# Forgetting attention in pairs of short and long query blocks, products in groups of four banks, TensorE order pinned

## Chip, core and metric

One Trainium2 chip (trn2); the program runs on one of its cores. The metric is the device time of one execution in microseconds (us), median of the runs. A difference of 0.2% (5 us) is about what a measurement of this kernel can tell from no change.

## The reference, cut to what matters

A decoder layer: a hybrid mixer (forgetting attention beside a gated linear attention), cross-attention into 256 memory tokens, a mixture of experts. The change is in the forgetting attention alone: 8 heads of 64 columns over 2048 positions, in float32.

```python
c = jnp.cumsum(log_sigmoid(f_logit), axis=-1)
for blk in range(S // 128):
    q0, q1 = blk * 128, blk * 128 + 128
    s = einsum('bhqd,bhkd->bhqk', q[:, :, q0:q1], k[:, :, :q1]) * d ** -0.5
    s = s + c[:, :, q0:q1, None] - c[:, :, None, :q1]
    p = softmax(where(causal, s, -inf), axis=-1)
    outs.append(einsum('bhqk,bhkd->bhqd', p, v[:, :, :q1]))
```

Query block qb (0 to 15) looks at (qb+1)*128 keys, so the work of a block grows sixteenfold over a head.

## The kernel before, in words

The program is a chain of stages. Stage 1 projects the input and leaves queries and keys in DRAM (`fqk_d`), the cumulated gates in `c_d`, values in `fv_d`. Stage 2 (`stage2`, from L456) is the forgetting attention. Stage 3 projects the result, and so on to the experts.

The order of instructions on each engine is not that of the source: a scheduler of the framework simulates the program and fixes one order per engine. Only what is marked `tc.keep_in_program_order` keeps its source order on its engine. Buffers (`bufs=n`) rotate, so an instruction that writes a tile waits for the last reader of the n-th tile before it.

Per head, `prep(h)` loads the head's queries `q2` and keys `k2` twice (both partition halves, [128,2048], L474, L475) and the gates `cr`, broadcast (L477); every second head the values of two heads (L482). In four chunks of 512 columns it splits queries and keys into high and low parts: R on ScalarE (L486) and VectorE (L487), L1 on ScalarE (L489), L2 on GpSimd (L490). R is triple-buffered, L1, L2 and cr double, q2 and k2 single. `prep` of head h+2 is started when head h ends.

Per query block, `scores` goes over banks of 512 keys: two matmuls R x L1 and R x L2 (L506, L507), on the last bank a third one that adds the causal mask (L509), into one of three PSUM banks `ps_s`. VectorE subtracts cr, takes the running maximum and writes the bank to SBUF (`sc`, five buffers of [128,2048]; L510); it negates the maximum (L515); ScalarE takes the exponentials in pieces of up to 1024 columns, with their sums (L518).

Per pair of query blocks, `values` goes over banks of two key blocks: up to four transposes into one of three PSUM banks `pt` (L536); the evacuation `t`, two of three on ScalarE (L541), one on VectorE (L539); then up to four products (L529) with the values (64 columns) as stationary operand, the two query blocks in the two column halves of the array, into `po`. The products of a bank are issued after the transposes of the next one. `close` copies `po` (L553, ScalarE), adds the sums and takes their reciprocal (L556, L557, L559), transposes back (`pn`, L562) and multiplies (L564); at the end of a head the normalisation goes over GpSimd (L571, L576) and out by DMA (L577).

Blocks are taken in order 0 to 15, head after head; the scores run four blocks ahead (`AHEAD = 4`), spread over the banks of `values` by a ratio of costs. From the fourth head on, free slots are given to `memory_in`, the preparation of the cross-attention (L744 to L774).

Of the kernel before, what the change touches and what calls it, by code (L numbers as in the profile page):

```python
# [25 lines left out]
def f32(ap):  # L26
    return ap.bitcast(F32)
# [18 lines left out]

def skip(gen, n):
    """gen, after n empty steps"""
    for _ in range(n):
        yield  # L50
    yield from gen


class Trunk:
# [9 lines left out]
    def split(self, hi, lo, src, scale=None):  # L64
        """hi + lo = src (* scale), each exact in a float32r"""
# [8 lines left out]
    def rstd(self, out, ss, mul, pool, eps=EPS, tag=""):  # L74
        """out = (ss * mul + eps) ** -0.5"""
# [19 lines left out]
    def consts(self):  # L95
# [8 lines left out]
        # -1e30 above the diagonal (row q, column k > q)  # L104
# [5 lines left out]
        with self.tc.tile_pool(name="vrows", bufs=1) as rp, self.tc.tile_pool(name="ps_c", bufs=1, space=PSUM) as pp:  # L110
# [10 lines left out]
            # blank lists for the routing  # L121
# [7 lines left out]
    def stage1(self):  # L129
# [3 lines left out]
        with tc.tile_pool(name="xT", bufs=1) as xp, tc.tile_pool(name="w1", bufs=2) as wp, \  # L133
                tc.tile_pool(name="ps1", bufs=2, space=PSUM) as pp:
            xh, xl = zip(*[[xp.tile([128, KT, 512], F32R, name=f"x{n}{c}") for n in "hl"] for c in range(4)])
            # the narrow columns: forget logits at 0..7, GLA gate inputs at 32..47
# [22 lines left out]
            def ttype(ws, m, c, dst):  # L159
                """rows m*128.. of the group's transposed product, tokens of chunk c"""  # L160
# [21 lines left out]
            with tc.tile_pool(name="xin", bufs=2) as ip, tc.tile_pool(name="psx1", bufs=2, space=PSUM) as px:  # L182
                xn = [[] for _ in range(4)]

                def prenorm(c):
                    """load and normalise chunk c"""
# [11 lines left out]
                def turn(c):  # L198
                    """chunk c transposed: yields after each bank"""
# [10 lines left out]
                def narrow(c):  # L210
# [6 lines left out]
                    # c: the running sum of log sigmoid(forget logit)  # L217
# [110 lines left out]
    def gla(self, gp, pp):  # L328
# [19 lines left out]
        for g in range(S // G):  # L348
# [3 lines left out]
            for p in range(2):  # L352
# [9 lines left out]
                # log decay, summed within chunks (16 times the reference's, taken off in the exps)  # L362
# [29 lines left out]
                # scores within chunks, level by level  # L392
# [13 lines left out]
                # within blocks of 8: factors of both signs about the block's middle, bounded as each  # L406
                # step's decay is held at exp(-17), under a float32's resolution beside the diagonal
# [10 lines left out]
                # between the halves of blocks of 2h, about the first half's end  # L418
# [28 lines left out]
                # the queries' factor 1/8 is in here: (o / 8) / sqrt(mean(o^2) / 64 + eps)  # L447
# [9 lines left out]
    def stage2(self):  # L457
        nc, tc = self.nc, self.tc
        with tc.tile_pool(name="fx", bufs=1, reuse_waits="tile") as fp, \
                tc.tile_pool(name="psx", bufs=2, space=PSUM, reuse_waits="tile") as pp:  # L460
            vs, heads, n_evac = {}, {}, [0]
            # in the order in which the last head lets go of them, for the stage that follows
            big = {}
            for nm in ("q2", "k2", "R0", "L10", "L20", "cr0", "R2", "R1", "L11", "L21", "cr1"):
                big[nm] = lambda nm=nm: fp.tile([128, S], F32R if nm[0] in "RL" else F32, name=nm)
            XW = 1024

            def prep(h):
                if h >= 8:
                    return  # L470
                q2, k2 = big["q2"](), big["k2"]()
                dma = nc.sync.dma_start if h == 1 else nc.gpsimd.dma_start
                for d in (slice(0, 64), slice(64, 128)):
                    dma(q2[d], self.fqk_d[h])  # L474
                    dma(k2[d], self.fqk_d[8 + h])  # L475
                R, L1, L2, cr = big[f"R{h % 3}"](), big[f"L1{h % 2}"](), big[f"L2{h % 2}"](), big[f"cr{h % 2}"]()
                dma(cr, bcast_rows(self.c_d, S, h * S))  # L477
                # [q hi; q lo] over 8 against [k hi; k hi] and [k lo; k lo]
                heads[h] = R, L1, L2, cr
                if h % 2 == 0:  # L480
                    v = vs[h // 2] = fp.tile([128, NT, 128], F32, name="v", bufs=2)
                    nc.gpsimd.dma_start(v, self.fv_d[:, h * 64:h * 64 + 128].rearrange("(b k) d -> k b d", k=128))  # L482
                yield
                for c in range(4):
                    cs = slice(c * 512, (c + 1) * 512)
                    nc.scalar.activation(R[:, cs], q2[:, cs], AF.Copy, scale=0.125)  # L486
                    nc.vector.scalar_tensor_tensor(R[64:128, cs], q2[64:128, cs], 0.125, f32(R)[64:128, cs], op0=OP.mult, op1=OP.subtract)  # L487
                    yield
                    nc.scalar.activation(L1[:, cs], k2[:, cs], AF.Copy)  # L489
                    nc.gpsimd.tensor_tensor(L2[:, cs], k2[:, cs], f32(L1)[:, cs], OP.subtract)  # L490
                    yield

            def scores(u):
                """exp(s - max) of head h's query block, and its sums: yields after each bank"""
                h, qb = u["h"], u["qb"]
# [3 lines left out]
                sc = u["P"] = fp.tile([128, S], F32, name="sc", bufs=5)  # L499
                m = fp.tile([128, 5], F32, name="m", bufs=4)  # L500
                for i, c0 in enumerate(range(0, n, 512)):
# [4 lines left out]
                    nc.tensor.matmul(ps[:, :w], R[:, qs], L1[:, ks], start=True, stop=False)  # L506
                    nc.tensor.matmul(ps[:, :w], R[:, qs], L2[:, ks], start=False, stop=not diag)  # L507
                    if diag:
                        nc.tensor.matmul(ps[:, w - 128:w], self.identb, self.cmask, start=False, stop=True)  # L509
# [6 lines left out]
                for j, c0 in enumerate(range(0, n, XW)):  # L516
                    cs = slice(c0, min(n, c0 + XW))
                    nc.scalar.activation(sc[:, cs], sc[:, cs], AF.Exp, bias=m[:, 4:5], accum_out=u["l"][:, j:j + 1])  # L518
                yield

            def values(u0, u1):
                """the outputs of two query blocks, transposed, in the array's two column halves:
                yields after each bank"""
                qb, po = u0["qb"], u1["po"]
                v, d = vs[u0["h"] // 2], slice(u0["h"] % 2 * 64, u0["h"] % 2 * 64 + 64)

                def product(t, todo):
                    for i, (half, kb) in enumerate(todo):
                        nc.tensor.matmul(po[half * 64:half * 64 + 64], v[:, kb, d], t[:, i], start=kb == 0, stop=kb == qb + half)  # L529

                last = None
                for g0 in range(0, qb + 1, 2):
                    todo = [(half, kb) for kb in (g0, g0 + 1) for half in range(2) if kb <= qb + half]
                    pt = pp.tile([128, 4, 128], F32, name="pt", bufs=3)
                    for i, (half, kb) in enumerate(todo):
                        nc.tensor.transpose(pt[:, i], (u0, u1)[half]["P"][:, kb * 128:(kb + 1) * 128], self.ident)  # L536
                    t = fp.tile([128, 4, 128], F32, name="t", bufs=4)
                    if n_evac[0] % 3 == 1:
                        nc.vector.tensor_copy(t[:, :len(todo)], pt[:, :len(todo)])  # L539
# [1066 lines left out]
```

## Time and profile before

| what | value |
|---|---|
| three runs | 2484.33, 2485.76, 2489.12 us (median 2485.76) |
| profiled execution, span | 2482.5 us |
| TensorE (PE) busy | 2368.5 us, 95% |
| VectorE (DVE) busy | 1444.0 us, 58% |
| ScalarE (ACT) busy | 1087.4 us, 44% |
| GpSimd (POOL) busy | 451.5 us, 18% |
| DMA, mean | 133 GB/s |
| stage 2: first score matmul to last product | 728.74 to about 1227 us |

The span is the time from the first to the last instruction of one profiled execution; no other time is given for that execution, and it stands 3.3 us below the median of the runs. Matmuls are pipelined, so their durations in the timeline overlap: what a group of matmuls takes is read from the start of one row to the start of the next. PEclk is the granted clock of TensorE as a share of its full speed (2.4 GHz); its lower level is 1.2 GHz.

### The profile page before, as it was taken

The page shows a single profiled execution, that of the slowest core. Times are in us where ns is not written, and L with a number is a line of the kernel's source. Part 1 is how long each engine was busy: PE and PEld are TensorE (multiplying, and loading weights), DVE is VectorE, ACT ScalarE, POOL GpSimd, SP SyncE. Part 2 cuts the span into 40 slices and gives each one's busy share as a digit, 9 for nine tenths or more (in the row PEclk, how much of TensorE's full clock was granted, in tenths as well). Part 3 has the DMA queues.
Part 4 walks back from the last instruction along what each step waited for, and adds up shares of the span by engine and source line. Part 5 has one row for each costly group of instructions (what it writes and reads, how often), then busy time and mean ns, then how long its engine had stood idle before and what let it go on. Part 6 is the DMA issues. An engine that isn't in the chain of part 4 may idle for free. (4 is left out here: it accounts for less than half of the span.)

```text
span 2482.5 us, 46191 instructions
## 1 busy us (share of the span) xinstructions
PE 2368.5 (95%) x17849; PEld 2022.0 (81%) x17849; DVE 1444.0 (58%) x4096; ACT 1087.4 (44%) x2438; POOL 451.5 (18%) x460
## 2 busy tenths in 40 slices
PE   7999999999999999999999999999599999999996
PEld 5799999877776777777778888888499989889995
DVE  5321145455447777767542236656567868768775
ACT  6322123233236666666431035544344545454542
POOL 1000012122122222211100000111323233223231
PEclk9999999999999999999999999999799999999998
DMA  5232222332274223200174421111478888879783
GB/s 174 70 93 82 71 75 88 97 92 89 74 195 103 66 72 80 66 27 10 39 260 143 140 104 45 59 53 52 152 227 258 239 274 255 255 236 270 263 246 110
DMA packets 275218, 328.99 MB, mean 133 GB/s; under 512 B 30774, under 2 KB 223088, under 8 KB 271921
## 3 DMA queue, kind: packets, MB, share of 16 engines
q1 hardware_dynamic: 243968, 223.79, 28.9%
q0 software_dynamic: 31024, 102.20, 14.1%
q8 instruction: 141, 2.31, 0.4%
q14 instruction: 85, 0.69, 0.1%
HBM read 251.88 MB, written 84.30 MB: 135 GB/s over the span
## 5 line engine op out<-in xcount | busy, mean ns | idle before, releaser
L90 PE MATMUL gu<-xTh,wer 128*128 128x288 f32 x1024 | 305.4, 303 | 0.5 <-ACT xTh L68 0.5
L91 PE MATMUL gu<-xTl,wer 128*128 128x288 f32 x1024 | 304.7, 298 | 0.0
L92 PE MATMUL gu<-xTh,wer 128*128 128x288 f32 x1024 | 303.8, 297 | 0.0
L69 DVE TENSOR_TENSOR wer<-wes,wer 128x1024 fp32r<-128x1024 f32 x192 | 232.2, 1220 | 35.3 <-ACT wer L68 34.4
L68 ACT ACTIVATE wer<-wes 128x1024 fp32r<-128x1024 f32 x192 | 197.7, 1052 | 108.8 <-PE yd L92 42.5
L90 PE MATMUL ps_mm<-w1r,xh 128*128 128x256 f32 x768 | 219.3, 286 | 0.0
L91 PE MATMUL ps_mm<-w1r,xh 128*128 128x256 f32 x768 | 218.7, 285 | 0.0
L92 PE MATMUL ps_mm<-w1r,xl 128*128 128x256 f32 x768 | 217.9, 284 | 0.0
L90 PEld LDWEIGHTS gu<-xTh,wer 128*128 128x128 f32 x1024 | 193.9, 190 | 3.7 <-ACT xTh L68 0.9
L92 PEld LDWEIGHTS gu<-xTh,wer 128*128 128x128 f32 x1024 | 194.9, 190 | 1.8
L91 PEld LDWEIGHTS gu<-xTl,wer 128*128 128x128 f32 x1024 | 194.9, 190 | 1.5
L518 ACT ACTIVATE sc<-sc,m 128x1024 f32<-128x1024 f32 (+2 forms) x192 | 170.9, 892 | 51.2 <-DVE m L515 51.0
L536 PE MATMUL pt<-ident,sc 128*128 128x128 f32 x1088 | 177.8, 289 | 7.3 <-DVE rc L556 3.7
L529 PE MATMUL po<-t,v 128*64 128x128 f32 x2176 | 178.3, 287 | 0.0
L529 PEld LDWEIGHTS po<-t,v 128*64 128x64 f32 x2176 | 124.1, 138 | 49.4 <-issue 21.7
L536 PEld LDWEIGHTS pt<-ident,sc 128*128 128x128 f32 x1088 | 126.6, 145 | 45.2 <-issue 28.3
L506 PE MATMUL ps_s<-L,R 128*128 128x512 f32 (+2 forms) x320 | 140.4, 440 | 15.8 <-DVE m L510 11.1
L90 PE MATMUL ps_mm<-xh,w1r 128*128 128x512 f32 x384 | 153.8, 403 | 0.0
L92 PE MATMUL ps_mm<-xh,w1r 128*128 128x512 f32 x384 | 153.0, 398 | 0.0
L91 PE MATMUL ps_mm<-xl,w1r 128*128 128x512 f32 x384 | 152.8, 398 | 0.0
L90 PEld LDWEIGHTS ps_mm<-w1r,xh 128*128 128x128 f32 x768 | 147.2, 192 | 3.8 <-issue 1.9
L510 DVE CUSTOM_DVE_ANT_0 sc<-ps_s,cr,m 128x512 f32<-128x512 f32 (+2 forms) x192 | 124.3, 647 | 44.4 <-PE ps_s L507 31.6
(405 smaller groups left out, 5780.3 us busy)
## 6 DMA issues: line engine op xcount, KB each, us to landing
wes<-in_w_expert_down_dram SPq DMA_DIRECT2D x64, 512.0 KB
wes<-in_w_expert_gate_dram SPq DMA_DIRECT2D x62, 512.0 KB
wes<-in_w_expert_up_dram SPq DMA_DIRECT2D x62, 512.0 KB
yr_d<-ye SPq DMA_DIRECT2D x32, 512.0 KB
w1s<-in_w_in_dram SPq DMA_DIRECT2D x96, 128.0 KB
xt<-in_x_dram SPq DMA_DIRECT2D x16, 512.0 KB
fqk_d<-o SPq DMA_DIRECT2D x32, 256.0 KB
h_d<-x POOLq DMA_DIRECT2D x16, 512.0 KB
```

What stands on the lines that cost most here:

```text
L68: nc.scalar.activation(hi, src, AF.Copy)
L69: nc.vector.tensor_tensor(lo, src, f32(hi), OP.subtract)
L90: mm(ps, ah, bh, start=start, stop=False)
L91: mm(ps, ah, bl, start=False, stop=False)
L92: mm(ps, al, bh, start=False, stop=stop)
L506: nc.tensor.matmul(ps[:, :w], R[:, qs], L1[:, ks], start=True, stop=False)
L510: nc.vector.tensor_tensor_reduce(out=sc[:, ks], in0=ps[:, :w], in1=cr[:, ks], scale=1.0, scalar=m[:, i - 1:i] if i else -3e38, op0=OP.subt ...
L518: nc.scalar.activation(sc[:, cs], sc[:, cs], AF.Exp, bias=m[:, 4:5], accum_out=u["l"][:, j:j + 1])
L529: nc.tensor.matmul(po[half * 64:half * 64 + 64], v[:, kb, d], t[:, i], start=kb == 0, stop=kb == qb + half)
L536: nc.tensor.transpose(pt[:, i], (u0, u1)[half]["P"][:, kb * 128:(kb + 1) * 128], self.ident)
```

## The change

The query blocks of a head are taken in pairs (2j, 2j+1) in the order j = 0, 7, 1, 6, 2, 5, 3, 4, so that a short pair and a long one alternate. A bank is transposed and evacuated as before, but its products wait in a list: once six banks are in it, the products of the oldest four are issued in a row (15 or 16 matmuls), also across pairs. For this `t` has eight buffers. The scores' lookahead is one pair and a half: at the end of pair n, pair n+1 and the first half of pair n+2 are scored. Transposes, products and scores (but for the first pair's scores) are pinned to source order on TensorE. The score buffers become three of [128,1024] and three of [128,2048]; q2 and k2 shrink to halves of [128,1024] columns, each still with one buffer, so that the second half is loaded only when the first has been read. The rest of the program keeps its order.

```diff
+    PAIRS = (0, 7, 1, 6, 2, 5, 3, 4)
+    BATCH, LAG = 4, 2
...
             def prep(h):
...
-                q2, k2 = big["q2"](), big["k2"]()
...
+                for g in range(2):
+                    gs = slice(g * 1024, (g + 1) * 1024)
+                    q2, k2 = (fp.tile([128, 1024], F32, name=nm) for nm in ("q2", "k2"))
+                    for d in (slice(0, 64), slice(64, 128)):
+                        dma(q2[d], self.fqk_d[h, :, gs])
+                        dma(k2[d], self.fqk_d[8 + h, :, gs])
+                    if g == 0:
+                        dma(cr, bcast_rows(self.c_d, S, h * S))
...
                     yield
+                    for c in range(2):
+                        ls, cs = slice(c * 512, (c + 1) * 512), slice(g * 1024 + c * 512, g * 1024 + (c + 1) * 512)
+                        nc.scalar.activation(R[:, cs], q2[:, ls], AF.Copy, scale=0.125)
...
+            def scores(u, half):
...
-                sc = u["P"] = fp.tile([128, S], F32, name="sc", bufs=5)
+                sc = u["P"][half] = fp.tile([128, S if long else 1024], F32, tag=f"sc{long}", name="sc", bufs=3)
...
-                    nc.tensor.matmul(ps[:, :w], R[:, qs], L1[:, ks], start=True, stop=False)
-                    nc.tensor.matmul(ps[:, :w], R[:, qs], L2[:, ks], start=False, stop=not diag)
+                    put = (lambda x: x) if u is pairs[0] else pin
+                    put(nc.tensor.matmul(ps[:, :w], R[:, qs], L1[:, ks], start=True, stop=False))
+                    put(nc.tensor.matmul(ps[:, :w], R[:, qs], L2[:, ks], start=False, stop=not diag))
...
+            def turn(u, g):
...
+                    pin(nc.tensor.transpose(pt[:, i], u["P"][half][:, kb * 128:(kb + 1) * 128], self.ident))
+                t = fp.tile([128, 4, 128], F32, name="t", bufs=self.BATCH + self.LAG + 2)
...
+            def product(u, t, todo):
...
+                    pin(nc.tensor.matmul(u["po"][half * 64:half * 64 + 64], v[:, kb, d], t[:, i], start=kb == 0, stop=kb == qb + half))
+                if todo[-1] == (1, qb + 1):
+                    pending.append(close(u))
...
+            for n, u in enumerate(pairs):
+                ratio = (n_banks(n + 1, 1) + n_banks(n + 2, 0)) / (u["j"] + 1)
                 due = 0.0
+                for g in range(u["j"] + 1):
                     due += ratio
+                    while due > 0.5 and not (done(n + 1, 2) and done(n + 2, 1)):
                         next(F, None)
                         due -= 1
+                    late.append(turn(u, g))
+                    if len(late) >= self.BATCH + self.LAG:
+                        for _ in range(self.BATCH):
+                            product(*late.pop(0))
```

In the new file the lines are: scores L520, L521, L523; reduction L524; negation L529; exponential L532; transposes L542; evacuation L545 and L547; products L558; `ot` L566; `pn` L575; queries and keys L488, L489; R L498 and L499; L1 L501; L2 L502.

**Place 1.** TensorE in the middle of a long pair of the second head, before (`po<-t,v` are products, `pt<-ident,sc` transposes):

```order
L529 MATMUL po<-t,v 64x128 x4
L536 MATMUL pt<-ident,sc 128x128 x7
L506 MATMUL ps_s<-L_8163,R_8162 128x512
L507 MATMUL ps_s<-L_8164,R_8162 128x512
L529 MATMUL po<-t,v 64x128 x3
L536 MATMUL pt<-ident,sc 128x128 x4
```

and the changed kernel in a later head:

```order
L542 MATMUL pt<-ident,sc 128x128 x3
L520 MATMUL ps_s<-L_10445,R_10444 128x512
L521 MATMUL ps_s<-L_10446,R_10444 128x512
L542 MATMUL pt<-ident,sc 128x128 x4
L558 MATMUL po<-t,v 64x128 x15
```

Over the stage, before has 219 groups of products (126 of 4 products, 47 of 3), the changed kernel 72 (48 of 15, 16 of 16, 8 of 14).

**Place 2.** TensorE at the longest pair, j = 7, of a head in the changed kernel, with buffer numbers: `sc_10406` is the pair's second half, `ps_s_10420` was its last score bank, `ps_s_10431` and `ps_s_10459` belong to later blocks:

```order
L520 MATMUL ps_s_10431<-L11_9680,R0_9679 128x384
L521 MATMUL ps_s_10431<-L21_9681,R0_9679 128x384
L523 LDWEIGHTS identb_65
L523 MATMUL ps_s_10431<-cmask_67,identb_65 128x128
L542 MATMUL pt_10438<-ident_63,sc_10297 128x128
L542 MATMUL pt_10438<-ident_63,sc_10316 128x128 x2
L520 MATMUL ps_s_10459<-L11_9680,R0_9679 128x512
L521 MATMUL ps_s_10459<-L21_9681,R0_9679 128x512
L523 LDWEIGHTS identb_65
L523 MATMUL ps_s_10459<-cmask_67,identb_65 128x128
L542 MATMUL pt_10466<-ident_63,sc_10333 128x128
L542 MATMUL pt_10466<-ident_63,sc_10406 128x128
```

and VectorE at the same place (`m` is the running maximum; ISA is the reduction):

```order
L524 ISA sc_10429,m_10430<-ps_s_10431,cr1_9682 128x384
L524 ISA m_10430 128x1
L524 ISA sc_10406,m_10407<-ps_s_10420,cr1_9682,m_10407 128x512
L524 ISA m_10407 128x1
L529 TENSOR_SCALAR m_10430<-m_10430 128x1
L524 ISA sc_10457,m_10458<-ps_s_10459,cr1_9682 128x512
L524 ISA m_10458 128x1
L529 TENSOR_SCALAR m_10407<-m_10407 128x1
```

Before, 31 rows stand on TensorE between the last score bank of block 15 of the second head and the first transpose of it; now 11 do. Its maximum is negated behind the reduction of a bank of another block.

**Place 3.** ScalarE where the next head's scores begin, before (L11 and R1 of the coming heads, `ot` of the pair that ends):

```order
L541 ACTIVATE t_9458<-pt_9453 128x512
L489 ACTIVATE L11_9880<-k2_9874 128x512 x4
L486 ACTIVATE R1_10638<-q2_10632 128x512 x4
L518 ACTIVATE sc_9392,l_9339<-sc_9392,m_9393 128x1024 x2
L518 ACTIVATE sc_9462,l_9461<-sc_9462,m_9463 128x128
L541 ACTIVATE t_9500<-pt_9495 128x512
```

and now:

```order
L501 ACTIVATE L11_9680<-k2_9684 128x512 x2
L498 ACTIVATE R1_10444<-q2_10448 128x512 x2
L547 ACTIVATE t_9507<-pt_9502 128x512
L532 ACTIVATE sc_9470,l_9400<-sc_9470,m_9471 128x1024
L532 ACTIVATE sc_9470,l_9400<-sc_9470,m_9471 128x256
L566 ACTIVATE ot_9525<-po_9435 128x128
```

The eight splits in a row have become two bursts of four (the second comes some seven rows later), and `ot` stands behind the first burst, an evacuation and two exponentials.

## Rows read from the trace of the kernel before

**Rows 1.** The page, part 1: busy time, share of the span, instructions.
```profile
PE 2368.5 (95%) x17849; PEld 2022.0 (81%) x17849; DVE 1444.0 (58%) x4096; ACT 1087.4 (44%) x2438; POOL 451.5 (18%) x460
```

**Rows 2.** Windows of stage 2: length, busy per engine, granted clock, DMA.
```profile
core 0: us, PE busy (x) PEld busy (x) DVE busy (x) ACT busy (x) POOL busy (x), PEclk, DMA share, GB/s
787.00:1224.00 437.00, 423.14 (x3659) 317.32 (x3658) 309.44 (x1027) 277.76 (x621) 76.13 (x73) 0.97 0.21 52
1040.00:1102.00 62.00, 60.35 (x509) 45.15 (x509) 42.40 (x152) 38.49 (x88) 10.17 (x10) 0.94 0.15 39
```

**Rows 3.** Waits of TensorE, 729 to 1228: total us, times, longest.
```profile
PE ps_s L506 <- DVE m L510: 11.1, 10, 2.1
PE pt L536 <- DVE rc L556: 3.7, 4, 1.1
PE pt L536 <- DVE mT L754: 2.6, 1, 2.6
```

**Rows 4.** Timeline of TensorE, full clock: start, us, what, idle before.
```profile
1218.03 0.66 PE L536 MATMUL pt<-ident,sc 128*128 128x128 f32 x4 [0.85 <-DVE rc L556]
1218.62 0.66 PE L529 MATMUL po<-t,v 128*64 128x128 f32 x8
1219.21 0.66 PE L536 MATMUL pt<-ident,sc 128*128 128x128 f32 x4
...
1220.38 1.53 PE L536 MATMUL pt<-ident,sc 128*128 128x128 f32 x12
1221.74 0.27 PE L562 MATMUL pn<-ident,ot 128*128 128x128 f32 x1
1221.95 1.97 PE L529 MATMUL po<-t,v 128*64 128x128 f32 x32
1223.85 0.55 PE L536 MATMUL pt<-ident,sc 128*128 128x128 f32 x3
```

**Rows 5.** Timeline of TensorE at the change to the fourth head.
```profile
913.69 0.50 PE L506 MATMUL ps_s<-L,R 128*128 128x512 f32 x1 [2.01 <-DVE m L510]
...
914.25 0.49 PE L536 MATMUL pt<-ident,sc 128*128 128x128 f32 x3
...
920.77 2.38 PE L536 MATMUL pt<-ident,sc 128*128 128x128 f32 x12
922.98 0.27 PE L562 MATMUL pn<-ident,ot 128*128 128x128 f32 x1
```

**Rows 6.** Groups by shape, 729 to 1228: VectorE and ScalarE, mean ns.
```profile
L518 ACT ACTIVATE sc<-sc,m 128x1024 f32<-128x1024 f32 x80 | 91.5, 1144 | 28.2 <-DVE m L515 28.2
L510 DVE CUSTOM_DVE_ANT_0 sc<-ps_s,cr,m 128x512 f32<-128x512 f32 x120 | 89.7, 747 | 35.7 <-PE ps_s L507 31.6 <-PE ps_s L509 1.6
L515 DVE TENSOR_SCALAR m<-m 128x1 f32<-128x1 f32 x128 | 18.6, 147 | 1.0
```

**Rows 7.** Timeline of ScalarE, splits for the fourth head.
```profile
905.72 2.19 ACT L489 ACTIVATE L<-k 128x512 fp32r<-128x512 f32 x4
907.82 2.18 ACT L486 ACTIVATE R<-q 128x512 fp32r<-128x512 f32 x4
```

**Rows 8.** Timeline of VectorE, low parts of R.
```profile
727.90 2.51 DVE L487 SCALAR_TENSOR_TENSOR R<-q,R 64x512 fp32r<-64x512 f32 x4
...
908.46 4.71 DVE L487 SCALAR_TENSOR_TENSOR R<-q,R 64x512 fp32r<-64x512 f32 x2 [0.41 <-ACT R L486]
...
913.66 0.69 DVE L487 SCALAR_TENSOR_TENSOR R<-q,R 64x512 fp32r<-64x512 f32 x1
```

**Rows 9.** Timeline of GpSimd, low parts of L, and DMA issues.
```profile
908.24 3.76 POOL L490 TENSOR_TENSOR L<-k,L 128x512 fp32r<-128x512 f32 x3
915.97 1.09 POOL L474 DMA_DIRECT2D q<-fqk_d  x2 [3.96 <-DVE m L515]
```

**Rows 10.** Windows while q2, k2 (and cr) are loaded; columns as in rows 2.
```profile
730.00:742.00 12.00, 12.00 (x74) 9.10 (x74) 10.50 (x41) 9.06 (x23) 0.00 (x0) 0.80 0.98 253
917.00:928.00 11.00, 11.00 (x97) 8.49 (x97) 3.40 (x11) 3.18 (x8) 1.07 (x3) 0.75 0.89 192
```

More of the change, by code (lines that the diff above doesn't have):

```diff
@@ L496, in scores @@
+            def scores(u, half):
+                h, qb = u["h"], 2 * u["j"] + half
                 n = (qb + 1) * 128
@@ L517, in scores @@
                     cs = slice(c0, min(n, c0 + XW))
-                    nc.scalar.activation(sc[:, cs], sc[:, cs], AF.Exp, bias=m[:, 4:5], accum_out=u["l"][:, j:j + 1])
+                    nc.scalar.activation(sc[:, cs], sc[:, cs], AF.Exp, bias=m[:, 4:5], accum_out=l[:, j:j + 1])
+                u["ready"] = half + 1
                 yield
[L521 to L539, printed above, removed]
-                    else:
-                        nc.scalar.activation(t[:, :len(todo)], pt[:, :len(todo)], AF.Copy)
-                    n_evac[0] += 1
-                    yield
-                    if last:
-                        product(*last)
-                    last = t, todo
-                yield
-                product(*last)
@@ new lines, in turn @@
+            def turn(u, g):
+                qb = 2 * u["j"]
+                todo = [(half, kb) for kb in (2 * g, 2 * g + 1) for half in range(2) if kb <= qb + half]
+                pt = pp.tile([128, 4, 128], F32, name="pt", bufs=3)
+                for i, (half, kb) in enumerate(todo):
+                    pin(nc.tensor.transpose(pt[:, i], u["P"][half][:, kb * 128:(kb + 1) * 128], self.ident))
+                t = fp.tile([128, 4, 128], F32, name="t", bufs=self.BATCH + self.LAG + 2)
+                if n_evac[0] % 3 == 1:
+                    nc.vector.tensor_copy(t[:, :len(todo)], pt[:, :len(todo)])
+                else:
+                    nc.scalar.activation(t[:, :len(todo)], pt[:, :len(todo)], AF.Copy)
+                n_evac[0] += 1
+                return u, t, todo
@@ new lines, in product @@
+            def product(u, t, todo):
+                h, qb = u["h"], 2 * u["j"]
+                if "po" not in u:
+                    u["po"] = pp.tile([128, 128], F32, tag="po", name="po", bufs=2)
+                v, d = vs[h // 2], slice(h % 2 * 64, h % 2 * 64 + 64)
+                for i, (half, kb) in enumerate(todo):
+                    pin(nc.tensor.matmul(u["po"][half * 64:half * 64 + 64], v[:, kb, d], t[:, i], start=kb == 0, stop=kb == qb + half))
+                if todo[-1] == (1, qb + 1):
+                    pending.append(close(u))
@@ L604, in stage2 @@
             F = first()
-            pending = []
-            AHEAD = 4
             side = prep(1)
-            while not units[AHEAD - 2].get("ready"):
+            while not (done(0, 2) and done(1, 1)):
                 next(F)
-            for i in range(0, len(units), 2):
-                u0, u1 = units[i:i + 2]
-                u1["po"] = pp.tile([128, 128], F32, tag="po", name="po", bufs=2)
-                target = units[min(i + AHEAD, len(units) - 1)]
-                cost = lambda j: sum((w["qb"] + 4) // 4 for w in units[j:j + 2])
-                ratio = cost(min(i + 2, len(units) - 2)) / (u0["qb"] // 2 + 2)
+            pending, late = [], []
+            for n, u in enumerate(pairs):
+                ratio = (n_banks(n + 1, 1) + n_banks(n + 2, 0)) / (u["j"] + 1)
                 due = 0.0
-                for _ in values(u0, u1):
+                for g in range(u["j"] + 1):
                     due += ratio
-                    while due >= 1 and not target.get("ready"):
+                    while due > 0.5 and not (done(n + 1, 2) and done(n + 2, 1)):
                         next(F, None)
                         due -= 1
+                    late.append(turn(u, g))
+                    if len(late) >= self.BATCH + self.LAG:
+                        for _ in range(self.BATCH):
+                            product(*late.pop(0))
                     if pending:
@@ L626, in stage2 @@
                         pass
-                    elif u0["h"] > 2:
+                    elif u["h"] > 2:
                         next(mem, None)
-                while not target.get("ready"):
+                while not (done(n + 1, 2) and done(n + 2, 1)):
                     next(F, None)
-                pending.append(close(u1))
-                if u1["qb"] == NT - 1:
+                if u["j"] == self.PAIRS[-1]:
                     for _ in side:
                         pass
-                    side = prep(u1["h"] + 2)
+                    side = prep(u["h"] + 2)
+            while late:
+                product(*late.pop(0))
             for g in pending:
```

75 lines of the change are left out of this document (30 added, 45 removed).

## The prediction, made before the changed kernel was run

> **What bounds the kernel now.** I read the page's busy line first: TensorE is busy 95% of the span, VectorE 58%, ScalarE 44% [rows 1]. So a gain has to come out of TensorE's own work, its waits or its clock, and a loss comes from a new wait on it. Then the windows of stage 2: over 437 us from 787 to 1224 TensorE is busy 423 us, VectorE 309 and ScalarE 278, at a mean granted clock of 0.97 [rows 2]. No other engine is near its limit; each has about a third of the stage free. The waits of TensorE over the whole stage are short: 11.1 us in ten waits of the first score matmul for VectorE's reduction (a score bank not yet free), 3.7 us for `rc` and 2.6 us for a copy of the memory side work [rows 3]. A reader should see that some 17 us of waits and the clock are all that is to be had besides the work itself.
>
> The work itself shows in the timeline [rows 4]. Four transposes take 0.59 us from their start to the next group's, eight products another 0.59. In long runs they are cheaper: 32 products take 1.90 us, so 24 more than eight cost 1.31, or 0.055 each; twelve transposes take 1.36, eight more than four cost 0.77, or 0.096 each. What is left of the short groups (0.59 - 8 x 0.055 = 0.15 and 0.59 - 4 x 0.096 = 0.21) is the price of going over from 128-column to 64-column work and back: up to **0.36 us for each group of products**. If I take the long runs whole (1.90/32 and 1.36/12, with their own changes inside), it is 0.11 + 0.14 = 0.25.
>
> **The change, part by part**, against the profiled execution of 2482.5 us, which stands 3.3 us below the median.
>
> *Fewer groups.* The order has 219 groups of products before and 72 after (place 1), 147 fewer. At 0.25 to 0.36 us that is 37 to 53 us; I take 0.29, nearer the low end since TensorE waits for somebody at some of these borders anyway: **-43**. TensorE's matmuls are otherwise the same in number and shape.
>
> *Old waits go.* The waits for the reduction come where four short blocks in a row start a head: their banks have less TensorE work than VectorE work. With short and long pairs alternating, those and the ones for `rc` lose their cause: 11.1 + 3.7 us [rows 3], **-15**; the 2.6 for the side work stay.
>
> *Old clock losses.* A clock of 0.97 over 437 us means that 2 x 0.03 x 437 = 26 us ran at 1.2 GHz. Twelve transposes then took 2.21 us (920.77 to 922.98) instead of 1.36 [rows 4, 5], so 38% of it, 10 us, was lost; such a stretch began behind a 2.01 us wait at a head's start [rows 5]. With those waits gone most of this comes back: **-8** (0 to -10).
>
> *New waits in the pair j = 7* (place 2). TensorE's order is now fixed, and three places of a head have a transpose of a half whose scores were finished just ahead. At j = 7, five score banks come in a row. One bank takes TensorE 0.56 us (913.69 to 914.25) [rows 5], VectorE 0.75 and 0.08 for the read-out; so VectorE falls behind by some 0.4 us, and then the reduction of another block's bank (0.75) stands ahead of the negation (0.15), and the first exponential takes 1.14 [rows 6]. From the last bank to the transpose that is 0.4 + 0.75 + 0.15 + 1.14 = 2.4 us in which TensorE has nothing that it may do. At j = 6 and j = 5 one reduction less is in the way and one bank of scores lies beside: 0.15 + 1.14 less a part of 0.56, or 1.1 to 1.2 each. A head: 4.7; eight heads 37.6, less one of 2.4 that I count with the start: **+35**. If only j = 7 counts and VectorE keeps up, it is 8 x 2.0 = 16; if ScalarE does another exponential first in all of them, 45.
>
> *New waits at a head's start* (place 3). `ot` now stands behind four splits (4.19 us took eight, from 905.72 to 910, so 2.1 for four) [rows 7], an evacuation and exponentials, and TensorE's fixed order has `pn` ahead of the next scores. Four splits (2.1), the evacuation (some 0.5) and the exponentials of 1024 and 256 columns (1.14 [rows 6] and some 0.5) make 4.2 us, of which TensorE's own rows ahead of `pn` cover about 2; so `pn` comes 2.2 us late in the five heads after which both kinds of splits follow, and 1.2 in the sixth: 12. The second half of R hangs on a DMA that is issued only when the first half of q2 has been read, behind cr: 2 MB came at 192 GB/s in 11 us [rows 10], so half of it takes 5.4 and cr as long; this reaches TensorE with 0.8 to 1.75 us, five times 1.3, or 6.5. VectorE's low parts of R: alone 0.69, but two took 4.71 beside GpSimd's low parts of L (3.76 for three) [rows 8, 9]. Now two of L lie in a row instead of three or four, so I expect about 2.5 for two; the three score banks hide all but 0.7 of it, five times 3.5. Sum 22, of which some overlaps: **+20** (10 to 30).
>
> The Trainium skill (SBUF — State Buffer, section "Who interferes with whom") says that a VectorE instruction with two SBUF inputs contends for a port pair with a GpSimd instruction that reads SBUF, and that the loser blocks fully. The row of 4.71 agrees with it. By the rule VectorE's burst ends when GpSimd's does; if it did not hold, the 3.5 us of that sentence would be none.
>
> *Start of the stage.* Before, R's four low parts were done by 730.4 [rows 8] because whole q2 and k2 had been loaded in stage 1. Now the second half of q2 waits until the first has been read, about 729.2. The queues are then full: 253 GB/s moved from 730 to 742 [rows 10], mostly the next head's loads. The pair j = 7 is second in the order and needs this half at once: some 5 us until it lands and is split (0.5 MB at 253 GB/s is 2.1, its issue about 1 per pair [rows 9], the split 0.5 and 0.7), 1.7 for two of L at 1.25 on GpSimd [rows 9], and 5 to 6 where ScalarE has next-head splits, which wait for their own load, ahead of the exponentials: **+12** (3 to 18).
>
> *New clock losses.* Waits of over 2 us come back in 13 places instead of about three. If a quarter of these sets the clock back as at 913 (some 7 us at the lower level, 38% of it lost, 2.7 us), it is **+9** (0 to +30).
>
> Sum: -43 - 15 - 8 + 35 + 20 + 12 + 9 = +10. From 2482.5 that is 2492.5 for such an execution, and **2496** for the median.
>
> Edits that cost nothing by themselves: the score buffers in two sizes, `t` with eight buffers, the halved DMAs (bytes as before, twice the issues on a GpSimd that is busy 76 of 437 us [rows 2]). The evacuations and exponentials are the same in number; ScalarE's 278 us of 437 cover them as long as TensorE isn't behind them in order, which is the case priced above.
>
> **The rivals.** *R1, faster.* The waits of place 2 are mostly covered. For it: VectorE has 30% free [rows 2], so it may not be behind at all, and then the reduction and a piece of the exponential lie beside transposes of other pairs. Of the 35 then 18 stay, of the head starts 10, of the start 10, of the clock 2: -66 + 40 = -26, or 2460. The point: less than 25 us of the new waits of places 2 and 3 together. Against it: the order of the rows leaves TensorE no other work there. Chance 0.37.
> *R2, much slower.* Each new wait over 2 us sets the clock back, as at 913 [rows 5]: 13 times 2.7 is 35 instead of 9, which gives 2522; for it speaks the window of 0.94 [rows 2] with only one such wait. Chance 0.14.
> *R3, no change.* The terms cancel, within 5 us of 2486: 0.13.
> *The forecast:* 0.36. That the change doesn't do what it says is not open as to the groups (the order has 72), but their price is: at half of 0.29 (a border that costs only where the next weights are late) the sum is 21 us higher, 2517, part of R2's side.
>
> **How the numbers follow.** Faster by over 0.2% (under 2481): R1, 0.37. Within 0.2%: 0.13. Slower (over 2491): 0.36 + 0.14 = 0.50. The forecast's own range is 2491 to 2515. The range over all cases goes from 2456 (R1, a little beyond its value) to 2528 (R2); what is left out is R1 with the full price of 0.36 and few waits, and R2 with the half price together.
>
> **What would show it.** After: products in runs of 14 to 16 that take 0.9 to 1.0 us; transposes at j = 7 with a wait for the exponential of 2 to 2.7 us, eight times, and smaller ones twice a head; waits of `pn` for `ot`; a gap in TensorE of about 5 us near 732 and another near 745; the ten waits for the reduction gone; a granted clock in the stage not above 0.97. Wrong: if TensorE's waits in stage 2 sum to less than 40 us, the time is below 2481 and R1 holds; if the stage's windows show 0.94 or less throughout, R2. If neither, and the runs of products aren't shorter by 40 us in all, the price of a group was wrong.

## The result, and the profile after

Four runs of the changed kernel give a median of 2507.3 us (2502.52 to 2512.1) beside 2486.11 us for the kernel before: ratio **1.0095, 95% interval 1.0072 to 1.0117**, slower by some 21 us. The profiled execution has a span of 2508.9 us. The busy line of the page, which answers to [rows 1]:

```profile
PE 2343.5 (93%) x17849; PEld 2034.0 (81%) x17849; DVE 1433.1 (57%) x4096; ACT 1088.6 (43%) x2438; POOL 472.1 (19%) x488
```

TensorE runs the same number of instructions with 25 us less busy time, and yet the span is longer: what the groups saved was lost in idle time. The windows of stage 2 (columns as in [rows 2]), first the whole stage of the changed kernel, then its first 61 us:

```profile
726.00:1257.00 531.00, 454.22 (x4112) 370.92 (x4113) 348.63 (x1174) 326.48 (x722) 109.11 (x120) 0.95 0.22 59
...
726.00:787.00 61.00, 42.04 (x328) 32.96 (x329) 36.37 (x113) 34.95 (x73) 15.13 (x19) 0.86 0.38 104
```

and the same stage of the kernel before:

```profile
729.00:1227.00 498.00, 479.57 (x4111) 358.87 (x4110) 358.50 (x1174) 321.86 (x717) 90.95 (x89) 0.97 0.24 60
```

From the first score matmul to the last `pn` of the stage it is now 531.0 us, before 498.8. The waits of TensorE in the stage (total, times, longest), to be held against [rows 3]:

```profile
PE pt L542 <- ACT sc L532: 45.6, 25, 4.8
PE pn L575 <- ACT ot L566: 13.6, 10, 2.7
PE ps_s L520 <- DVE R L499: 11.5, 2, 8.6
PE ps_s L520 <- DVE m L524: 7.5, 10, 1.6
PE pt L542 <- DVE t L545: 0.3, 1, 0.3
```

The wait of the pair j = 7 in the third head shows how it comes about. TensorE (start, duration, what, idle before and its releaser):

```profile
876.03 0.50 PE L520 MATMUL ps_s<-L,R 128*128 128x512 f32 x1
876.37 0.39 PE L521 MATMUL ps_s<-L,R 128*128 128x512 f32 x1
876.61 0.23 PE L523 MATMUL ps_s<-cmask,identb 128*128 128x128 bf16 x1
876.67 0.28 PE L542 MATMUL pt<-ident,sc 128*128 128x128 f32 x1
879.78 0.44 PE L542 MATMUL pt<-ident,sc 128*128 128x128 f32 x2 [2.83 <-ACT sc L532]
```

VectorE and ScalarE in the same time:

```profile
876.37 0.68 DVE L586 TENSOR_REDUCE fss<-sq 128x8 f32<-128x512 f32 x1
876.97 0.74 DVE L524 CUSTOM_DVE_ANT_0 sc<-ps_s,cr,m 128x512 f32<-128x512 f32 x1
...
877.70 0.68 DVE L524 CUSTOM_DVE_ANT_0 sc<-ps_s,cr 128x512 f32<-128x512 f32 x1
...
878.31 0.27 DVE L529 TENSOR_SCALAR m<-m 128x1 f32<-128x1 f32 x2
...
877.82 0.61 ACT L532 ACTIVATE sc<-sc,m 128x384 f32<-128x384 f32 x1 [0.83 <-DVE m L529]
...
878.49 1.15 ACT L532 ACTIVATE sc<-sc,m 128x1024 f32<-128x1024 f32 x1
```

The half's own last bank is reduced at 876.97, then another block's bank at 877.70, only then come the negations (878.31) and the exponential (878.49 to 879.6); TensorE stands from 876.9 to 879.78. This is the queue that place 2 shows. In this head two more instructions stand ahead in it: a reduction of the head's normalisation on VectorE (L586, 0.68 us) and another block's exponential on ScalarE (877.82). From the second head on j = 7 cost 2.2 to 3.6 us, j = 6 0.97 to 1.11 and j = 5 1.45.

At the start of the stage (TensorE again):

```profile
726.13 0.47 PE L520 MATMUL ps_s<-L,R 128*128 128x128 f32 x2 [2.83 <-DVE R L499]
...
735.62 0.80 PE L520 MATMUL ps_s<-L,R 128*128 128x512 f32 x1 [8.65 <-DVE R L499]
742.31 0.50 PE L520 MATMUL ps_s<-L,R 128*128 128x512 f32 x1 [1.04 <-DVE m L524]
744.49 0.44 PE L520 MATMUL ps_s<-L,R 128*128 128x384 f32 x1 [0.77 <-DVE m L524]
751.10 1.76 PE L542 MATMUL pt<-ident,sc 128*128 128x128 f32 x7 [4.79 <-ACT sc L532]
```

8.65 + 1.04 + 0.77 + 4.79 = 15.3 us of idle time in the first 25 us of the stage.

### The profile page after: what moved, and what is told of

The parts are those of the page before. It is cut to its first block, busy times and chain, and to the rows that moved or that the text cites. A ratio compares the mean times of both kernels' runs of the same rounds, so it can differ in the third digit from the quotient of the medians.

```text
span 2508.9 us, 46269 instructions
## 1 busy us (share of the span) xinstructions
PE 2343.5 (93%) x17849; PEld 2034.0 (81%) x17849; DVE 1433.1 (57%) x4096; ACT 1088.6 (43%) x2438; POOL 472.1 (19%) x488
## 5 line engine op out<-in xcount | busy, mean ns | idle before, releaser
L542 PE MATMUL pt<-ident,sc 128*128 128x128 f32 x1088 | 172.0, 283 | 45.9 <-ACT sc L532 45.6
L532 ACT ACTIVATE sc<-sc,m 128x1024 f32<-128x1024 f32 (+3 forms) x192 | 171.1, 892 | 54.9 <-DVE m L529 53.0
L542 PEld LDWEIGHTS pt<-ident,sc 128*128 128x128 f32 x1088 | 129.7, 146 | 72.5 <-ACT sc L532 53.1
L524 DVE CUSTOM_DVE_ANT_0 sc<-ps_s,cr,m 128x512 f32<-128x512 f32 (+1 forms) x192 | 124.4, 648 | 69.6 <-PE ps_s L523 53.7
L520 PE MATMUL ps_s<-L,R 128*128 128x512 f32 (+2 forms) x320 | 145.1, 454 | 19.8 <-DVE R L499 11.5
L547 ACT ACTIVATE t<-pt 128x512 f32<-128x512 f32 (+1 forms) x192 | 105.8, 560 | 110.9 <-PE pt L542 110.9
L558 PE MATMUL po<-t,v 128*64 128x128 f32 x2176 | 149.1, 285 | 0.0
```

The lines of the kernel that those rows point to most:

```text
L520: put(nc.tensor.matmul(ps[:, :w], R[:, qs], L1[:, ks], start=True, stop=False))
L524: nc.vector.tensor_tensor_reduce(out=sc[:, ks], in0=ps[:, :w], in1=cr[:, ks], scale=1.0, scalar=m[:, i - 1:i] if i else -3e38, op0=OP.subt ...
L542: pin(nc.tensor.transpose(pt[:, i], u["P"][half][:, kb * 128:(kb + 1) * 128], self.ident))
L547: nc.scalar.activation(t[:, :len(todo)], pt[:, :len(todo)], AF.Copy)
L558: pin(nc.tensor.matmul(u["po"][half * 64:half * 64 + 64], v[:, kb, d], t[:, i], start=kb == 0, stop=kb == qb + half))
```

## The experiments

My theory went into them as: the pinned order, by where it puts the last score bank of a half, makes the waits. The rival: the alternation of short and long pairs makes them. All ratios are to the kernel before on the same chip. "Waits" and "clock" are of TensorE in stage 2, waits without the one ahead of its first matmul; "stage" runs from the first score matmul to the last `pn`.

| kernel | order, pins | groups | ratio (95%) | stage us | waits us | clock |
|---|---|---|---|---|---|---|
| before | natural, none | 219 | 1 | 498.8 | 18.8 | 0.97 |
| the change | alternating, all | 72 | 1.0095 (1.0072 to 1.0117) | 531.0 | 75.7 | 0.95 |
| e1_batch1 | alternating, all | 280 | 1.021 (1.0193 to 1.0227) | 554.9 | 45.8 | 0.97 |
| e2_free_scores | alternating, scores free | 112 | 1.0001 (0.9988 to 1.0014) | 499.2 | 36.3 | 0.95 |
| e3_natural | natural, all | 72 | **0.9824** (0.9807 to 0.984) | 461.8 | 22.8 | 0.98 |
| e4_ahead | alternating, all, earlier scores | 72 | 1.0006 (0.9993 to 1.0019) | 503.9 | 54.9 | 0.95 |
| e5_two_halves | alternating, all, two q2, k2 | 72 | 1.0166 (1.0142 to 1.019) | 539.9 | 86.8 | 0.94 |
| e6_five_long | alternating, all | 72 | 1.012 (1.0089 to 1.0151) | 528.5 | 77.6 | 0.95 |
| e7_natural_single | natural, all | 285 | 1.006 (1.0042 to 1.0079) | 517.2 | 22.2 | 0.99 |
| e8_natural_free | natural, scores free | 109 | 0.9846 (0.9822 to 0.9871) | 459.2 | 18.5 | 1.00 |
| e9_natural_no_pin | natural, none | 263 | 0.9935 (0.9911 to 0.9959) | 488.1 | 2.0 | 1.00 |
| e10_first_head_natural | first head natural, then alternating | 72 | 1.0066 (1.0044 to 1.0087) | 519.9 | 63.7 | 0.95 |
| e11_natural_again | as e3 | 72 | 0.9818 (0.9806 to 0.9831) | 457.1 | 22.2 | 0.99 |
| e12_natural_six | natural, all | 48 | 1.001 (0.9998 to 1.0022) | 502.7 | 59.0 | 0.97 |

**e3_natural: the order of the pairs.**

```diff
-    PAIRS = (0, 7, 1, 6, 2, 5, 3, 4)
+    PAIRS = (0, 1, 2, 3, 4, 5, 6, 7)
-                sc = u["P"][half] = fp.tile([128, S if long else 1024], F32, tag=f"sc{long}", name="sc", bufs=3)
+                sc = u["P"][half] = fp.tile([128, S], F32, tag="sc", name="sc", bufs=5)
```

> The changed kernel with the pairs in the order 0 to 7 (five score buffers of 2048 columns), all pins and the groups of four banks kept: 72 groups. Theory (the pin with a lookahead of a pair and a half makes the waits): each pair's second half is finished just ahead of its first transpose, so the waits for the exponential are at least as long, 45 to 75 us, and the time is 2505 to 2540. Rival (the alternation makes the waits): they fall below 15 us and the time is 2465 to 2480.

The rival was right: 0.9824, 2438.5 us, faster than both kernels and than the rival's own 2465 to 2480; a second set of runs gave 0.9818 (0.9806 to 0.9831). Its waits of TensorE:

```profile
PE pt L542 <- DVE rc L569: 9.3, 5, 1.9
PE pt L542 <- ACT sc L532: 7.9, 12, 2.5
PE ps_s L520 <- DVE R L499: 2.8, 1, 2.8
PE pn L575 <- ACT ot L566: 2.7, 8, 0.5
PE ps_s L520 <- DVE m L524: 1.7, 6, 0.4
```

The waits for the exponential fell from 45.6 to 7.9 us and those of `pn` from 13.6 to 2.7, with every pin in place. The two programs' orders (equal instructions in a row are one row) agree with this: between the last R x L2 matmul of a long pair's second half and its first transpose stand 13, 13, 17 and 22 rows of TensorE with alternation (j = 7, 6, 5, 4), and 22, 34, 35 and 29 in natural order. A short pair has one to four banks to transpose, and in that space the whole second half of the long pair behind it must be scored.

The largest wait left, 9.3 us put down to `rc`, is five waits of 1.9 us at changes of heads, and as I read the rows the label misleads. The transposes wait for one of the three `pt` banks, and VectorE evacuates it late, behind two low parts of R that ran beside GpSimd's low parts of L (two rows of VectorE, one of TensorE):

```profile
776.35 2.71 DVE L499 SCALAR_TENSOR_TENSOR R<-q,R 64x512 fp32r<-64x512 f32 x2 [0.18 <-ACT R L498]
...
779.88 0.68 DVE L545 COPY t<-pt 128x512 f32<-128x512 f32 x1
...
780.61 0.66 PE L542 MATMUL pt<-ident,sc 128*128 128x128 f32 x4 [1.88 <-DVE rc L569]
```

The evacuation ends at 780.56 and the transposes start 0.05 us later.

**e6_five_long: the buffers alone** (the second line of the edit above, order as in the change).

> Control: the changed kernel with the score buffers of the run in natural order (five of 2048 columns instead of three short and three long), pairs alternating as in the change. Theory (the alternation, not the buffers, made the difference between the two orders): ratio 1.008 to 1.011, waits for the exponential 40 to 50 us. Rival (the three buffers of each size were the cause): waits below 20 us and ratio 0.99 or below.

1.012, just above my interval of 1.008 to 1.011, and 44.9 us of waits for the exponential: the buffers are not the cause, so e3's gain is the order's.

**e4_ahead: the long pair scored earlier.**

```diff
-                sc = u["P"][half] = fp.tile([128, S if long else 1024], F32, tag=f"sc{long}", name="sc", bufs=3)
+                sc = u["P"][half] = fp.tile([128, S if long else 1024], F32, tag=f"sc{long}", name="sc", bufs=4 if long else 3)
-                t = fp.tile([128, 4, 128], F32, name="t", bufs=self.BATCH + self.LAG + 2)
+                t = fp.tile([128, 4, 128], F32, name="t", bufs=self.BATCH + self.LAG + 1)
+                full = n + 2 < len(pairs) and pairs[n + 2]["j"] > 3
+                upto = lambda: done(n + 1, 2) and done(n + 2, 2 if full else 1)
-                ratio = (n_banks(n + 1, 1) + n_banks(n + 2, 0)) / (u["j"] + 1)
+                ratio = (n_banks(n + 1, 1) * (u["j"] > 3) + n_banks(n + 2, 0) + n_banks(n + 2, 1) * full) / (u["j"] + 1)
-                    while due > 0.5 and not (done(n + 1, 2) and done(n + 2, 1)):
+                    while due > 0.5 and not upto():
```

> The changed kernel with a fourth long score buffer (seven buffers of t instead of eight) and the scores of a long pair finished by the end of the long pair before, a short pair ahead of it; order, pins and 72 groups kept. Theory (it is the position of the last score bank that makes the waits): waits for the exponential fall from 45.6 to 15 us or less, those of pn for ot (13.6) and of the start (11.5) stay, the time is 2470 to 2482. Rival (VectorE and ScalarE can't keep up, the waits only move to the score banks): waits of the stage stay above 65 us, 2498 to 2510.

1.0006 (2484.5 us), some 22 us better than the change but short of what I expected: waits for the exponential fell to 25.5, not below 15, and those for a free score bank rose from 7.5 to 13.1. The waits of the stage, 54.9 us, lie between the two forecasts: the position of the last bank is a part of the mechanism, and a part of what is won there comes back at the score banks.

**e2_free_scores: scores not pinned.**

```diff
-                    put = (lambda x: x) if u is pairs[0] else pin
+                    put = lambda x: x
```

> The changed kernel with the scores' matmuls not pinned on TensorE (transposes and products still are): the scheduler may move them ahead; 112 groups of products instead of 72. Theory (the waits of transposes for the exponential, 45.6 us, come from where the pinned order puts the last score bank of a long pair): they fall below 15 us, 40 more groups cost 8 to 10, the time is 2480 to 2495. Rival (the alternation of short and long pairs makes the burst whatever the pin): waits stay at 35 us or more, 2507 to 2520.

As forecast in time (1.0001), and the waits for the exponential are 4.5 us. So the pin of the scores has a part in those 45.6 us: either the natural order or free scores take most of them away. But now TensorE waits 23.1 us for score banks: with alternation the burst is there in any case, and VectorE has to take it.

**e1_batch1, e7_natural_single and e9_natural_no_pin: the price of a group.** e1 and e7 set `BATCH, LAG = 1, 1` with eight buffers of `t`, e1 in the alternating, e7 in the natural order. e9 is e3 with `pin = lambda x: x`.

> The changed kernel with the products of one bank at a time (BATCH 1, LAG 1; eight buffers of t as before): 280 groups of products instead of 72, everything else of the change kept. Theory (a group costs about 0.25 us, since the changed kernel's stage got 32 us longer while its waits grew by 60 and its clock lost some 8): 208 more groups cost 40 to 51 us, so 2547 to 2558. Rival (a group costs only the two steps of 0.093 us that the trace shows at its borders): 39 us at most, with part of it inside the waits that exist, so 2527 to 2546. Rival (grouping is worth nothing): 2502 to 2512.

> Natural order of pairs, pins kept, products of one bank at a time (285 groups instead of 72; five score buffers as in the natural run). Theory (a group costs 0.25 to 0.30 us, the price that the two pairs of runs so far give): 213 groups cost 53 to 64 us, so 2491 to 2503 against 2438.5, ratio 1.004 to 1.009. Rival (a group costs only two steps of 0.093 us): 40 us, ratio 0.998. The kernel before, with 219 groups and no pin, lies at 1.000.

> Natural order, products still issued four banks in a row in the source, but nothing pinned on TensorE: the scheduler breaks the groups up, 263 of them instead of 72. Theory (the pin is worth what it keeps together, 0.25 to 0.30 us a group): 191 groups cost 48 to 57 us, less up to 15 us of waits that the scheduler avoids, ratio 0.995 to 1.005 against 0.9824 with the pins. Rival (the free order makes up for the groups by itself): ratio 0.985 or below.

e1 came to 2535.3 us, below my 2547 to 2558 and inside the first rival's interval. But its waits for the exponential fell to 21.5 us, which I had not allowed for; that a slower TensorE waits less is my reading. So, after the result, I take the work as stage less waits less 40% of the time at 1.2 GHz (the time is 2 x (1 - clock) x stage; the share lost in it, 38% in the prediction, is rounded): 434 us for the change, 496 for e1, 432 for e3, 491 for e7, 486 for e9, 468 for before. That gives 62/208 = 0.30, 59/213 = 0.28 and 54/191 = 0.28 us a group; before against the change 34/147 = 0.23. e7 was run with this price as its forecast, and its ratio, 1.006, lies inside the 1.004 to 1.009 expected and above the rival's 0.998. e9 differs from e3 in the pins as well as in the groups. e9's ratio of 0.9935 is just below the interval that I had given it, and it has next to no waits:

```profile
PE ps_s L520 <- DVE R L499: 2.8, 1, 2.8
PE pn L575 <- ACT ot L566: 1.1, 2, 0.8
PE ps_s L520 <- DVE m L524: 0.7, 1, 0.7
PE pt L542 <- ACT sc L532: 0.2, 1, 0.2
```

The pins alone, in natural order, are worth 0.9935 to 0.9824, some 27 us: by the sums above 54 us of groups kept whole, less the waits and clock that they bring.

**e8_natural_free: natural order, scores free** (e3 with e2's edit).

> Natural order, groups of four banks, scores not pinned (109 groups as the scheduler splits some). Theory (in this order the pin of the scores costs no wait and only keeps groups whole): 37 more groups cost 9 to 11 us, waits change by less than 10 us, ratio 0.984 to 0.990 against 0.9824. Rival (the pin still makes waits, 25.6 us in the natural run): waits fall to 15 us or less and the ratio is 0.980 or below.

0.9846, inside the theory's interval, and its own interval overlaps that of e3. 37 more groups cost 9 us of work (0.24 each), and fewer waits and a clock of 1.00 give it back: the stage takes 459.2 us beside 461.8 in e3 and 457.1 in e11.

**e5_two_halves: the start, by buffers.**

```diff
-                    q2, k2 = (fp.tile([128, 1024], F32, name=nm) for nm in ("q2", "k2"))
+                    q2, k2 = (fp.tile([128, 1024], F32, name=nm, bufs=2) for nm in ("q2", "k2"))
```

and seven buffers of `t`, as in e4.

> The changed kernel with two buffers for the halves of q2 and k2 (and seven of t instead of eight), so that both halves of the first head are loaded before the stage starts; order 0, 7, 1, 6, ... and all else kept. Theory (the single half-buffers cost the start some 13 us, and add little later): the first transpose comes 5 to 8 us into the stage instead of 18.9, the waits for R (11.5) and the 4.8 us wait for the exponential at the start go, the other waits stay; ratio to the kernel before 1.003 to 1.006 instead of 1.0095 (10 to 16 us less). Rival (the start waits for loads on full queues in any case): first transpose after 15 us or more, ratio 1.008 to 1.011. Second rival (the second halves also make the waits of pn in later heads): 20 us or more less, ratio 1.001 or below.

Slower: 1.0166, outside all three forecasts. The first transpose comes 27.4 us into the stage instead of 18.9, and the waits of `pn` rose from 13.6 to 20.2 us. The second halves were now issued before the stage (GpSimd), but ScalarE still waited for them:

```profile
716.10 0.52 POOL L488 DMA_DIRECT2D q<-fqk_d  x1
```

```profile
742.34 2.19 ACT L498 ACTIVATE R<-q 128x512 fp32r<-128x512 f32 x4 [12.79 <-DMA q<-fqk_d]
```

and TensorE:

```profile
745.56 0.79 PE L520 MATMUL ps_s<-L,R 128*128 128x512 f32 x1 [17.30 <-DVE R L499]
```

The window of that time:

```profile
712.00:745.00 33.00, 12.74 (x57) 10.20 (x55) 7.73 (x27) 6.66 (x15) 9.01 (x12) 0.73 0.91 263
```

263 GB/s over 33 us are 8.7 MB, at a DMA share of 0.91; the next head's queries and keys, cr and both v's are among them. But the first halves went out later too. Their second load was issued by GpSimd at 712.83 here, and at 701.36 in the changed kernel:

```profile
712.83 0.53 POOL L489 DMA_DIRECT2D k<-fqk_d  x1 [11.36 <-PE ps_mm L92]
...
701.36 0.52 POOL L489 DMA_DIRECT2D k<-fqk_d  x1
```

From 700 to 712 us the DMA share is therefore 0.40 instead of 0.81, and between 700 and 745 both kernels move the same 10 MB. The first rival is right in that loads were waited for while the DMA was busy, though not in the size; whether the buffers or this later issue made the start late isn't separated.

**e10_first_head_natural: the start, by order.** The control e6 with the first head's pairs taken as 0, 1, 2, 3, 5, 6, 7, 4.

> The control with five score buffers (ratio 1.012), but the first head's pairs in the order 0, 1, 2, 3, 5, 6, 7, 4, so that the second half of its queries and keys is needed later; heads two to eight alternate as in the change. Theory (the start costs the change some 18 us of waits, 11 for R, 4.6 for the exponential, 2 for score banks, and is a matter of the order alone): the first transpose comes about 4 us into the stage, the wait for R falls below 4 us, ratio 1.002 to 1.006. Rival (the loads are late in any case and the wait only moves): R's wait stays above 8 us, ratio 1.009 or more.

1.0066 against e6's 1.012, some 13 us, with intervals that just don't overlap; the profiled stages differ by 8.6. R's wait is 2.8 us, the first transpose comes 4.1 us into the stage. So the start cost some 9 to 13 us and was the order's doing; the interval that I gave was a little too hopeful, as the first head is not free of waits (two of 1.6 and 1.7 us for score banks near 792).

**e11_natural_again and e12_natural_six: longer groups.** e12 is e3 with `BATCH, LAG = 6, 1` and six buffers of the sums `l`.

> The natural order with pins and groups of four banks once more, beside the run below. Ratio 0.980 to 0.985.

> Natural order, pins, products of six banks in a row once seven are transposed (nine buffers of t, six of the sums): 48 groups (40 of 23, 8 of 21) instead of 72. Theory (a group costs 0.28 us in the natural order too): 24 fewer are 7 us, ratio 0.003 below the run beside it. Rival (the longer run of products holds up the transposes that ScalarE and VectorE wait for, so that waits grow by as much or more): ratio equal or higher.

e11 lies in its interval (0.9818). e12 loses all of the gain, 1.001, as its rival had it. Its longest waits in sum:

```profile
PE pt L542 <- ACT sc L532: 33.2, 31, 2.4
PE pn L575 <- ACT ot L566: 7.2, 6, 3.2
PE ps_s L520 <- DVE m L524: 6.0, 10, 1.8
```

33 us of waits for the exponential came back. BATCH and LAG were changed together, so which of them brought the waits stays open. Nor did the work (as taken above) fall by the 7 us that I expected: 432 us with 48 groups as with 72. The price of a group holds between four products and fifteen; beyond that these runs show no gain.

## Why the prediction was right, and where it was off

The sign, the range and the places of the new waits held: 2496 forecast, 2507.3 measured, inside the forecast's own 2491 to 2515. Point by point:

- *New waits in the pairs j = 7, 6, 5:* forecast +35 in 23 places; measured 45.6 less 4.8 at the start and 1.8 at the last pair of the stage = 39.0 in 23. j = 7 took 2.24 or more in every head beside the 2.4 forecast, j = 6 mostly 0.97 and j = 5 1.45 beside 1.1 to 1.2. Right in place and nearly in size.
- *Head starts:* +20 forecast; measured 13.6 us of `pn` waiting for `ot`, ten times. At the six head changes named it is 8.8 us beside 12; where `ot` stood behind splits that waited for the second half of q2 it is 4.4 in three heads beside 6.5. The term of 3.5 for VectorE's low parts of R brought no wait of TensorE for R after the start. Two of them took 2.67 us beside two of GpSimd's and 1.29 without (two rows of VectorE in the changed kernel):

```profile
860.15 2.67 DVE L499 SCALAR_TENSOR_TENSOR R<-q,R 64x512 fp32r<-64x512 f32 x2 [0.70 <-ACT R L498]
869.63 1.29 DVE L499 SCALAR_TENSOR_TENSOR R<-q,R 64x512 fp32r<-64x512 f32 x2 [1.98 <-ACT R L498]
```

  I had expected 2.5, so the burst was right and what it costs TensorE was not. The Trainium skill (SBUF — State Buffer, "Who interferes with whom") says that a VectorE instruction with two inputs in SBUF contends with a GpSimd instruction that reads SBUF. These rows agree with it as [rows 8] do: GpSimd's two ran until 862.26 us, VectorE's until 862.82.
- *Start of the stage:* +12 forecast, 15.3 us of idle time measured, and 9 to 13 by e6 against e10.
- *All waits:* 18.8 to 75.7 us is +57; the forecast's terms for waits (-15 + 35 + 20 + 12) make +52. Of the old waits' -15 only part came: `rc` is gone, but the first score matmul still waits for the reduction, 7.5 us in ten places beside 11.1 [rows 3].
- *R1* needed less than 25 us of new waits in places 2 and 3; there were 52.6 (39.0 + 13.6).
- *Clock:* -8 and +9 forecast, nothing in sum. Measured 0.95 over 531 us, 53 us at 1.2 GHz instead of 30; at 40% of it about +9. **Mis-sized**: the net loss grew by some 9 us, where the two terms nearly cancelled. The records don't tell old losses from new ones. Ten waits of over 2 us came instead of 13, and the window of 0.94 on which R2 leaned had none (its longest are 1.7 and 0.9 us).
- *Fewer groups:* -43 forecast, 34 measured between these two kernels (0.23 each), **mis-sized** by 9 us; e1, e7 and e9 gave 0.28 to 0.30, close to the 0.29 that I took, and e8 0.24. Why some pairs of kernels show less isn't shown; the subtraction of 40% is rough.
- *Runs of products* were to take 0.9 to 1.0 us; fifteen take 1.9 (756.35 to 758.25 in the first head). The timeline counts each product twice (2176 rows for 1088 products), so the prediction's "32 products" are 16. The price of a group, a difference of times, is not touched by this.

57 + 9 - 34 = 32 us is what the stage grew (498.8 to 531.0); it closes by construction, as the 34 is what is left when waits and clock are taken off. The forecast had the stage 10 us longer, so it missed by 22, and all three groups of terms missed to the same side. The rest of the program was some 6 us shorter in this execution (2482.5 - 498.8 = 1983.7 before, 1977.9 after), which no term of the forecast covers and which leaves the 26 us between the spans; the medians differ by 21. That the median came within 11 us of the forecast is in this part luck.

One reason was only half right. I blamed the pins for the waits of place 2 ("TensorE's order is now fixed"). e3 keeps the pins and has few of the waits, so the pins alone don't make them; e2 keeps the alternation, frees the scores and has few of them too, at the price of waits for score banks. With groups of four banks the waits for the exponential need both, and the alternation costs waits either way; with groups of six they come in natural order as well (33.2 us in e12). Another reason did not hold: I said of the old waits that the alternation takes their cause away. With it the waits for the reduction still come to 7.5 us; in natural order they go further down, to 1.7 us in e3 and 0.7 in e9.

## What to carry to other kernels

Taking products of 64 columns in groups of fifteen instead of four saves TensorE 0.23 to 0.30 us for each group fewer here, and pinning its order keeps the groups whole. Groups of 23 showed no further saving and brought waits back. In a pinned order, count for every consumer how much work of the engine stands between the last piece of its input and itself, and hold it against the chain behind (here a reduction, a negation and an exponential, 2 us): with groups of four banks neighbours of nearly equal size left room here, a short unit ahead of a long one did not. A change of several parts is best tried with one part undone: this one held a gain of 1.8% (e3) and a loss of 2.7% (the change against e3).

## What I had not expected of the hardware

- Loads that were issued earlier landed later. With two buffers (e5) R's second half was issued at 716.1 us and reached ScalarE at 742.3; with one it was issued at 726.9 and reached it at 733.6. The DMA share was 0.91 from 712 to 745 in e5 and 0.74 in the change. That e5 also issued most of its first halves 11 us later is not separated from this.
- Without pins, 263 groups and 2.0 us of waits (e9) ran at a clock of 1.00 over 488 us, the change with 72 groups and 75.7 us of waits at 0.95, a loss of about 9 us more than before by the 40% taken above. In the change all eleven stretches at 1.2 GHz after the first 20 us of the stage begin inside a wait of 1.4 us or more or within 1.5 us behind it, as at 815.8 us behind the wait that ends at 814.52. But 15 of its 26 such waits had no such stretch behind them, and one kernel with nearly the same waits (22.8 and 22.2 us) ran at 0.98 in e3 and 0.99 in e11. So short waits go with a lower clock here; which of them brings it down isn't shown.
